# The norm weight of a differential attention: multiplied into the gates, or into half the rows of the output weights

## The chip, the cores and the metric

The kernel runs on one core of a Trainium2 chip. A core has five engines that work side by side and wait for each other through semaphores: TensorE (PE in the profile, its weight loads PEld), VectorE (DVE), ScalarE (ACT), GpSimd (POOL) and SyncE (SP), which here issues nearly all transfers between the chip's memory and the on-chip buffers. The metric is the device time of one execution in microseconds (us), the median over runs; lower is better. Besides, one execution of each kernel was profiled, and its trace lists every instruction.

## The reference, cut to what matters

The reference is one step of a two-layer network on 1280 tokens (256 context, 1024 latent) of width 1024. Layer 0 has a convolution branch A and a differential attention B with 4 heads of 128 value channels; layer 1 has two grouped-query attentions. Each layer is an input projection, its branches, and an output projection. In layer 0 a head's output `o` is normalised over its 128 channels, multiplied by a norm weight `subln_g` (one number for each of the 128 channels, the same for all heads) and a constant, and by a gate of its own:

```
o = over_query_blocks(lambda qb: diff_attend(qb, keys, vals, lam), q)
o = rms_norm(o, subln_g) * (1.0 - lam_init)
o = o.reshape(b, T, B_W) * jax.nn.silu(b_z)
return jnp.concatenate([a, o], axis=-1) @ w_out, new_kv
```

`lam_init` is 0.2 in layer 0. The branches are concatenated, so columns 0 to 511 of the product's left side come from A and columns 512 to 1023 from B, head by head; `w_out` has 1024 rows to match. A factor that depends on the channel alone can therefore stand on the left side's column or on the matching row of `w_out`.

## The kernel before, in words

All work is in tiles of 128 tokens (ten of them, two of context and eight latent). Products that need full precision are made of three matmuls over a high and a low part of each operand; so each weight chunk is loaded, rounded by ACT to its high part, and the rest taken by a subtraction (`wcut`, `wo_chunk`).

**Input projection of layer 0** (`l0_in`, profile about 45 to 530 us). Seven groups of 512 output columns are run one after the other, group by group over the tokens (`run_group`). Four of the groups are heads (`head_units`). For each head and token tile `vz_done` (L507) takes the values and the gate from the product: ACT copies the value (L509), `silu2` makes the gate with a tanh on ACT and one DVE instruction (L339, L340), then DVE multiplies it by the tile `subg` (L513), and SP stores it to the tensor GZ0 in memory (L514). That is 40 times, for 4 heads and 10 tiles. Between the groups' units a filler runs the convolution and then the layer norm of branch A in five pairs of tiles (`ln_steps`, L557 to L598: loads of the convolution's result L569, DVE L574 to L581, POOL L583 and L584, ACT L582 and L585, DVE L586 and L587, store L588), and a second generator works out the next modulations. `subg` is set up once at the start (L1365 to L1367): the norm weight is loaded to all 128 partitions, 128 numbers in each, and multiplied by 0.4 (0.8 for the constant, and a half that `silu2` leaves out).

**First attention** (`l0_attn`, about 514 to 804 us). Its keys and first queries (`l0_keys` L646 to L653, `l0_query` L661) are loaded in the last part of the input projection, after two thirds of the last head's units (`freed0`), into memory that the projection has left. A head's gates come back from GZ0 in one load (L752). In `fin` DVE multiplies the normalised head output by the gate (L724), and SP writes it into the concatenated tensor CAT (L727).

**First output projection** (`out_proj`, about 802 to 955 us). The weights come in eight chunks of 128 rows (`wo_chunk`, L811): SP loads a chunk of 512 KB into a tile `wor` (L815), ACT rounds it half by half (L818), and POOL subtracts (L819). Chunks 0 to 2 are made during the attention, chunks 3 to 7 at the start of the projection (L844) through three slots, so that a further load waits until POOL is done with an earlier chunk. Chunks 4 to 7 are the rows 512 to 1023. The first two token tiles are projected together: for each chunk, PE makes two products with the high part of the token tile, by the weights' high (L852) and low part (L853), and one with its low part (L856). ACT then reads the two accumulators (L870), and POOL and DVE finish the tile. The token tiles are transposed in `prep` (L832 to L835).

**What sets the order.** The program text gives the dependences and a first order; the order in which each engine gets its instructions is then written out by a planner, which simulates the whole program with costs of its own and lets an instruction go when its operands are ready by that simulation (L1547: `schedule_with_timeline_sim=True`). At run time each engine works through its own list in that order; an instruction that has to wait holds up those behind it, and the same holds for the list of transfers that SP issues.

Of the kernel before, what the change touches and what calls it, by code (L numbers as in the profile page):

```python
# [10 lines left out]
F32 = mybir.dt.float32  # L11
# [3 lines left out]
ALU = mybir.AluOpType  # L15
# [17 lines left out]
def f32(ap):  # L33
    return ap.bitcast(F32)
# [42 lines left out]
class K:  # L77
# [323 lines left out]
    def l0_in(self, ws, raw, wp, cxp, p1, small, acc, pst, mod, freed):  # L401
        nc, a = self.nc, self.a
# [80 lines left out]
        def head_units(h):  # L483
# [23 lines left out]
            def vz_done(t, ps):  # L507
                v = small.tile([128, 128], F32, tag="vz", name=f"vz{h}_{t}")
                nc.scalar.copy(v, ps[:, 256:384])  # L509
                nc.sync.dma_start(self.V0[h, t], v)  # L510
                gz = small.tile([128, 128], F32, tag="gz", name=f"gz{h}_{t}")
                self.silu2(gz, ps[:, 384:512], small, f"z{h}_{t}")
                nc.vector.tensor_tensor(gz, gz, self.subg, ALU.mult)  # L513
                nc.sync.dma_start(self.GZ0[h, t], gz)  # L514
                return v

# [294 lines left out]
    def wo_chunk(self, l, k, pool, bufs=1):  # L811
        nc = self.nc
        w = pool.tile([128, 2, D], F32R, name=f"wo{l}_{k}")
        r = pool.tile([128, D], F32, tag="ac", bufs=bufs, name=f"wor{l}_{k}")
        nc.sync.dma_start(r, self.a["wo"][l, k])  # L815
        for n in range(2):
            s = slice(n * 512, n * 512 + 512)
            nc.scalar.copy(w[:, 0, s], r[:, s])  # L818
            nc.gpsimd.tensor_tensor(w[:, 1, s], r[:, s], f32(w[:, 0, s]), ALU.subtract)  # L819
        return w  # L820
# [411 lines left out]
def build(tc, a):  # L1232
    nc = tc.nc
    k = K(tc, a)
    with ExitStack() as ctx:
        cst = ctx.enter_context(tc.tile_pool(name="cst", bufs=1))
# [29 lines left out]
        def pool(c, name, bufs=1, **kw):  # L1266
            return c.enter_context(tc.tile_pool(name=name, bufs=bufs, **T, **kw))
# [41 lines left out]
        with ExitStack() as c1:  # L1309
# [9 lines left out]
            with ExitStack() as c2:  # L1319
                xp = pool(c2, "xp0", 3)  # L1320
                k.cond(cst, xp)

                def load(g):
                    t0, n = TGS[g]
                    xs = []
                    if g == 1:
                        quad = hp.tile([128, 4, D], F32, tag="lo2", name="x0_g1")
                    for t in range(t0 // 128, (t0 + n) // 128):
                        if g == 0:
                            x = xp.tile([128, D], F32, tag="x", bufs=2, name=f"x0_{t}")  # L1330
                        elif g == 1:
                            x = quad[:, t - t0 // 128]
                        else:
                            if t % 2 == 0:
                                pair = hp.tile([128, 2, D], F32, tag=("hi0", "lo0")[t % 4 // 2], name=f"x0_{t}")
                            x = pair[:, t % 2]
                        nc.sync.dma_start(x, a["x"][t])
                        xs.append(x)
                    return xs

                def norm(x, t):
                    junk = xp.tile([128, D], BF16, tag="junk", bufs=1, name=f"xj_{t}")
                    k.x_norm(x, junk, small, f"x{t}")

                xs = load(1)
                first = k.mod_steps(0, (0, 2, 1, 3), xp, wp, "w", small, psm, pst, cst, nc.vector, "xraw")
                for i in range(20):
                    next(first)
                    if i % 5 == 3:
                        norm(xs[i // 5], 2 + i // 5)  # L1350
                k.use_mod()
                k.h_group(0, 1, xs, hpr, xp, pst, range(4))
                for _ in first:
                    pass
                k.after = k.last
                k.h_group(0, 1, xs, hpr, xp, pst, range(4, 8))
                ws = k.wgroup(a["we"][0], raw, wp, "w0")
                with tc.issue_after(k.after):
                    k.ropeC = cst.tile([128, 8, 64], F32, name="ropeC")
                    nc.sync.dma_start(k.ropeC, a["ropec"])  # L1360
                    k.ropeS = cst.tile([128, 8, 64], F32, name="ropeS")
                    nc.sync.dma_start(k.ropeS, a["ropes"])
                    k.ropeT = hp.tile([128, 2, 1024], F32, name="ropeT")
                    nc.sync.dma_start(k.ropeT, a["ropet0"])
                    k.subg = cst.tile([128, 128], F32, name="subg")  # L1365
                    nc.sync.dma_start(k.subg, a["subg"].broadcast_to([128, 128]))
                    nc.vector.tensor_scalar(k.subg, k.subg, 0.4, None, ALU.mult)  # L1367
                    k.nsink = cst.tile([128, 8], F32, name="nsink")
                    nc.sync.dma_start(k.nsink, a["sink"].broadcast_to([128, 8]))
                    nc.vector.tensor_scalar(k.nsink, k.nsink, -1.0, None, ALU.mult)  # L1370
                    k.qn = cst.tile([128, 64], F32, name="qn")
                    nc.sync.dma_start(k.qn, a["qn"].broadcast_to([128, 64]))
                    k.kn = cst.tile([128, 64], F32, name="kn")
                    nc.sync.dma_start(k.kn, a["kn"].broadcast_to([128, 64]))
                    ls = cst.tile([128, 4], F32, name="ls")
                    lam = hp.tile([128, KC, 512], F32, tag="hi2", name="lam")[:, 0, 0:384].rearrange("p (v d) -> p v d", d=64)
                    lv, lp = lam[:, 0:4], lam[:, 4:6]
                    nc.sync.dma_start(lv, a["lamv"][None].broadcast_to([128, 4, 64]))
                    nc.vector.tensor_tensor(lp, lv[:, 0::2, :], lv[:, 1::2, :], ALU.mult)
                    nc.vector.tensor_reduce(ls[:, 0:2], lp, AX.X, ALU.add)  # L1380
                    nc.scalar.activation(ls[:, 0:2], ls[:, 0:2], AF.Exp)
                    k.nlam = ls[:, 3:4]
                    nc.vector.tensor_tensor(ls[:, 2:3], ls[:, 1:2], ls[:, 0:1], ALU.subtract)
                    nc.vector.tensor_scalar(k.nlam, ls[:, 2:3], -0.2, None, ALU.add)
                    for g in (2, 0):
                        xs = load(g)
                        for i, x in enumerate(xs):
                            norm(x, TGS[g][0] // 128 + i)
                        k.h_group(0, g, xs, hp, xp, pst, eng=nc.vector)
# [171 lines left out]
```

## Time and profile before

| | |
|---|---|
| median of 3 runs | 1828.43 us (1823.73 to 1829.55) |
| profiled execution, its own time | 1829.68 us |
| its span, first to last instruction | 1827.9 us |
| PE busy | 1727.2 us, 94% of the span |
| DVE busy | 1238.3 us, 68% |
| ACT busy | 971.6 us, 53% |
| POOL busy | 782.0 us, 43% |
| granted TensorE clock, mean | 0.985 |

Busy time is the time in which an engine had an instruction under way, waiting for a port or a buffer of the on-chip memory included. A row of a group of instructions names the line of the kernel, the engine, the operation, and what is written from what. In rows in order of time the first number is the start in us, the second the duration or, for several of a kind (x2), their common stretch; brackets give the idle time of the engine just before and what ended it.

### The profile page before, as it was taken

To read this page: it belongs to the slowest core of one execution; us is meant where nothing else is said; L and a number is where in the kernel's file an instruction comes from. 1 tells how busy PE (TensorE), PEld (TensorE's weight loads), DVE (VectorE), ACT (ScalarE), POOL (GpSimd) and SP (SyncE) were. 2 spreads that over 40 slices of the span, in tenths; PEclk is the share of its full clock that TensorE was granted. 3 is DMA by queue.
4 is the path that set the end of the run, shared out by engine and by line. 5 is a ranking of instruction groups with operands and counts; after the bars stand their busy time and mean duration, and the time that the engine had idled before them with its cause. 6 is when DMAs were issued, how large, how long until landed. Compare 5 with 4: busy or idle time off the path is not lost. (4 is left out here: it accounts for less than half of the span.)

```text
span 1827.9 us, 28289 instructions
## 1 busy us (share of the span) xinstructions
PE 1727.2 (94%) x9434; PEld 1419.5 (78%) x9434; DVE 1238.3 (68%) x2975; ACT 971.6 (53%) x2040; POOL 782.0 (43%) x696
## 2 busy tenths in 40 slices
PE   6999999999859999899999999998999999999998
PEld 2787788988747777778887778886888888878886
DVE  6657545674779999945566672118899989999322
ACT  6432244344337777753344543217778878898311
POOL 2322022222557777763237873203344334354332
PEclk9999999999979999999999999999999999999999
DMA  8457478785764433144146346254112114141441
GB/s 292 166 161 211 150 185 203 190 234 134 222 185 113 139 104 93 47 137 163 72 156 199 139 121 167 75 137 113 36 43 66 36 41 107 53 146 58 156 173 55
DMA packets 220086, 241.24 MB, mean 132 GB/s; under 512 B 72128, under 2 KB 154464, under 8 KB 219684
## 3 DMA queue, kind: packets, MB, share of 16 engines
q1 hardware_dynamic: 207284, 233.53, 43.1%
q0 software_dynamic: 1792, 3.15, 0.9%
q10 hardware_dynamic: 10864, 2.75, 0.8%
q8 instruction: 75, 1.23, 0.3%
q14 instruction: 71, 0.58, 0.1%
HBM read 169.08 MB, written 70.28 MB: 131 GB/s over the span
## 5 line engine op out<-in xcount | busy, mean ns | idle before, releaser
L397 ACT ACTIVATE E<-E,mm 128x1536 f32<-128x1536 f32 (+3 forms) x240 | 293.5, 1227 | 69.0 <-DVE E L394 58.4
L270 POOL TENSOR_TENSOR w_w<-raw_w,w_w 128x512 fp32r<-128x512 f32 x88 | 118.7, 1360 | 258.1 <-ACT w_w L269 244.0
L1217 PE MATMUL S<-k1d,q1s 128*128 128x512 f32 (+1 forms) x704 | 206.4, 389 | 4.5 <-DMA q1s<-qT 2.1
L372 POOL TENSOR_TENSOR el<-ef,eh 128x512 fp32r<-128x512 f32 x96 | 124.3, 1296 | 185.6 <-DVE eh L371 180.7
L394 DVE TENSOR_SCALAR_CACHE_REDUCE E<-S,mm 128x512 f32<-128x512 f32 x256 | 189.8, 744 | 11.5 <-PE S L777 3.0
L1147 PE MATMUL wt_et<-ident,E 128*128 128x128 f32 x1264 | 186.2, 273 | 3.2 <-ACT E L397 2.5
L1147 PEld LDWEIGHTS wt_et<-ident,E 128*128 128x128 f32 x1264 | 153.6, 140 | 37.3 <-ACT E L397 4.3
L777 PE MATMUL S<-kd,qs 128*128 128x512 f32 (+1 forms) x416 | 133.4, 431 | 30.2 <-DVE E L394 24.1
L368 DVE TENSOR_TENSOR el<-wt_et,eh 128x512 fp32r<-128x512 f32 x220 | 146.8, 682 | 10.0 <-ACT eh L367 9.3
L1217 PEld LDWEIGHTS S<-k1d,q1s 128*128 128x128 f32 x704 | 121.3, 190 | 28.5 <-DVE E L394 7.1
L367 ACT CAST eh<-wt_et 128x512 fp32r<-128x512 f32 x220 | 124.1, 594 | 30.4 <-PE wt_et L1147 29.9
L1142 PE MATMUL pv_pv<-el,v 128*128 128x512 f32 x316 | 138.8, 439 | 0.5 <-POOL el L372 0.2
L318 PE MATMUL acc_g<-w_w,hi 128*128 128x512 f32 x336 | 131.5, 393 | 1.8 <-DVE v L1000 1.3
L319 PE MATMUL acc_g<-w_w,hi 128*128 128x512 f32 x336 | 132.4, 394 | 0.5 <-POOL w_w L270 0.5
L320 PE MATMUL acc_g<-w_w,lo 128*128 128x512 f32 x336 | 131.6, 392 | 0.0
L1141 PE MATMUL pv_pv<-eh,v 128*128 128x512 f32 x316 | 128.3, 406 | 0.9 <-DVE eh L371 0.5
L852 PE MATMUL acc_po<-wo,oh 128*128 128x512 f32 x320 | 126.0, 395 | 0.6 <-DVE oy L724 0.6
L853 PE MATMUL acc_po<-wo,oh 128*128 128x512 f32 x320 | 125.1, 392 | 0.0
L394 DVE TENSOR_SCALAR_CACHE_REDUCE E<-S 128x512 f32<-128x512 f32 (+1 forms) x160 | 99.8, 629 | 18.7 <-PE S L1217 11.7
L777 PEld LDWEIGHTS S<-kd,qs 128*128 128x128 f32 x416 | 70.0, 197 | 51.6 <-DVE E L394 38.6
L856 PE MATMUL acc_po<-wo,ol 128*128 128x512 f32 x320 | 103.3, 393 | 0.0
L269 ACT CAST w_w<-raw_w 128x512 fp32r<-128x512 f32 x96 | 59.0, 621 | 82.8 <-DMA raw_w<-in_wod 23.3
(294 smaller groups left out, 4544.4 us busy)
## 6 DMA issues: line engine op xcount, KB each, us to landing
rawm_v<-in_wmodt SPq DMA_DIRECT2D x64, 256.0 KB, 3.1
raw_w<-in_we SPq DMA_DIRECT2D x56, 256.0 KB, 3.4
X<-AW SPq DMA_DIRECT2D x32, 336.0 KB, 5.5
qs<-QK SPq DMA_DIRECT2D x80, 128.0 KB, 2.8
ac<-CAT SPq DMA_DIRECT2D x20, 512.0 KB, 3.5
raw_w<-in_wod SPq DMA_DIRECT2D x40, 256.0 KB, 2.8
q1s<-qT SPq DMA_DIRECT2D x40, 256.0 KB, 2.6
xraw_m<-in_wmod SPq DMA_DIRECT2D x32, 256.0 KB, 4.8
```

The costliest lines, as they stand in the source:

```text
L318: nc.tensor.matmul(ps[:, o:], a, w[:, 0, o:], start=(k == 0), stop=False)
L319: nc.tensor.matmul(ps[:, o:], a, w[:, 1, o:], start=False, stop=False)
L320: nc.tensor.matmul(ps[:, o:], b, w[:, 0, o:], start=False, stop=(k == KC - 1))
L368: nc.vector.tensor_tensor(lo, ps, f32(hi), ALU.subtract)
L394: nc.vector.tensor_scalar(e[:, o : o + w], S, -1.0, init, ALU.mult, ALU.min, accum_out=m[:, i : i + 1])
L397: nc.scalar.activation(e[:, :n], e[:, :n], AF.Exp, bias=init, scale=-1.0, accum_out=s)
L777: nc.tensor.matmul(S, q[:, hl], kd[:, c, kofs + o : kofs + o + n], start=(hl == 0), stop=(hl == 1))
L852: nc.tensor.matmul(po[hn], oh[:, k, :], wo[k][:, 0, s], start=(k == 0), stop=False)
L1141: nc.tensor.matmul(pv, vs, wh, start=(i == 0), stop=False)
L1142: nc.tensor.matmul(pv, vs, wl, start=False, stop=(i == nk - 1))
L1147: nc.tensor.transpose(ps[:, g * 128 : g * 128 + 128], E[g][:, ec : ec + 128], self.ident)
L1217: nc.tensor.matmul(S, qs[:, g, :], kd[hl][:, kc : kc + n], start=(hl == 0), stop=(hl == 1))
```

## The change

The multiplication of the gates by `subg` is taken out. Instead each of the chunks 4 to 7 of the first output weights is multiplied, after its load and before it is split, by `subg` as one number for each partition (a partition of the chunk is a row of the weights, and so a channel of a head). `subg` becomes a column: 128 partitions with one number each, loaded as such, and still multiplied by 0.4. The stored gates and the head outputs in CAT are without the factor; the product is the same.

```diff
@@ head_units, vz_done
                 self.silu2(gz, ps[:, 384:512], small, f"z{h}_{t}")
-                nc.vector.tensor_tensor(gz, gz, self.subg, ALU.mult)
                 nc.sync.dma_start(self.GZ0[h, t], gz)
@@ wo_chunk
         nc.sync.dma_start(r, self.a["wo"][l, k])
+        if l == 0 and k >= 4:
+            nc.vector.tensor_scalar(r, r, self.subg, None, ALU.mult)
         for n in range(2):
@@ build
-                    k.subg = cst.tile([128, 128], F32, name="subg")
-                    nc.sync.dma_start(k.subg, a["subg"].broadcast_to([128, 128]))
+                    k.subg = cst.tile([128, 1], F32, name="subg")
+                    nc.sync.dma_start(k.subg, a["subg"].rearrange("o p -> p o"))
                     nc.vector.tensor_scalar(k.subg, k.subg, 0.4, None, ALU.mult)
```

## The prediction

> **What bounds the kernel now.** I read the page's span and busy times first, then a table of busy time by stage, and then, for the two stages that the edit touches, the instructions in order of time on each engine. The columns of the stage table are the stretch, its length, then the busy time of PE, PEld, DVE, ACT and POOL (number of instructions in brackets), the granted TensorE clock, the DMA share and GB/s.
>
> ```profile
> span 1827.9 us, 28289 instructions
> PE 1727.2 (94%) x9434; PEld 1419.5 (78%) x9434; DVE 1238.3 (68%) x2975; ACT 971.6 (53%) x2040; POOL 782.0 (43%) x696
> ...
> 250.00:480.00 230.00, 230.00 (x1607) 206.40 (x1606) 138.75 (x284) 98.68 (x252) 65.40 (x50) 1.00 0.72 184
> 480.00:530.00 50.00, 29.51 (x166) 26.19 (x164) 36.45 (x66) 16.34 (x45) 29.26 (x25) 0.80 0.68 212
> ```
>
> TensorE is the bound nearly everywhere, and from 250 to 480 us it has no gap at all: what another engine saves there can't shorten the span. The exception is the seam between the first input projection and the first attention, from 480 us on: 29.51 busy in 50. The gates' multiply (L513) lies across both, and the new multiply lands in the first output projection.
>
> ```profile
> L513 DVE TENSOR_TENSOR gz<-gz,subg x40: 254/291/6066, 259.9 to 519.1; 128x128 f32<-128x128 f32 x40
> ...
> 250.00:480.00 230.00, 17.64 (x34) 1.00 0.72 184
> 480.00:533.00 53.00, 7.33 (x7) 0.79 0.65 205
> ```
>
> The first row has the 40 removed instructions with their shortest, median and longest duration in ns: half of them take 291 or less, one took 6066. The other two are the same instructions by stage (DVE busy): 17.64 us lie under a full TensorE, 7.33 in the seam, 25.0 in all.
>
> **Part 1, the removal under a full TensorE.** 17.64 us of DVE time go from 250 to 480 us. They cost nothing now, because PE is busy 230 of these 230 us (rows above), so they give 0. If that cover were gone they would be worth their 17.64 at most; nothing else in the edit takes it away.
>
> **Part 2, the removal in the seam.** Here are the rows on which it turns, in order of time and from four engines; SPq is the queue of the engine that issues nearly all transfers.
>
> ```profile
> 477.72 6.07 DVE L513 TENSOR_TENSOR gz<-gz,subg 128x128 f32<-128x128 f32 x1
> 478.58 2.55 POOL L583 TENSOR_TENSOR lu<-lu,lncon 128x512 f32<-128x512 f32 x2
> 478.75 1.43 SPq L570 DMA_DIRECT2D azr<-AZ  x1
> 481.09 2.54 POOL L584 TENSOR_TENSOR lu<-lu,lncon 128x512 f32<-128x512 f32 x2
> 482.41 0.63 ACT L585 ACTIVATE lu<-lu 128x512 f32<-128x512 f32 x1 [4.02 <-POOL lu L584]
> 483.71 0.68 DVE L586 SCALAR_TENSOR_TENSOR lu<-lu 128x512 f32<-128x512 f32 x1
> 483.81 0.32 SPq L514 DMA_DIRECT2D GZ<-gz  x1
> 484.22 0.60 SPq L646 DMA_DIRECT2D kd<-QK  x1
> 485.51 0.61 SPq L651 DMA_DIRECT2D ck<-in_cbk  x1
> 489.49 0.68 DVE L495 TENSOR_TENSOR ch<-cn,ropeT 128x512 f32<-128x512 f32 x1
> 492.05 1.29 POOL L653 TENSOR_TENSOR kd<-ck,kd 64x512 fp32r<-64x512 f32 x1 [8.43 <-DMA qs<-QK]
> 493.42 2.50 POOL L499 TENSOR_TENSOR ch<-ch 128x512 f32<-128x512 f32 x2
> 495.38 1.09 DVE L501 TENSOR_TENSOR ch<-ch 128x512 fp32r<-128x512 f32 x1 [5.21 <-ACT ch L500]
> 500.90 1.12 PE L360 MATMUL tr_st<-ident,hl 128*128 128x128 f32 x4 [6.42 <-DVE hl L357]
> 505.23 1.06 DVE L513 TENSOR_TENSOR gz<-gz,subg 128x128 f32<-128x128 f32 x1
> 514.53 1.37 DVE L513 TENSOR_TENSOR gz<-gz,subg 128x128 f32<-128x128 f32 x1
> 517.31 0.85 SPq L569 DMA_DIRECT2D lu<-CV  x2
> 520.10 1.37 DVE L574 SCALAR_TENSOR_TENSOR lu<-lu,lncon 128x512 f32<-128x512 f32 x2 [0.74 <-DMA lu<-CV]
> 532.92 7.23 PE L777 MATMUL S<-kd,qs 128*128 128x512 f32 x18 [16.99 <-DVE E L394]
> ```
>
> The 6.07 us instruction needs no data after 477.7; it ends at 483.79, when POOL's four two-input instructions end (481.09+2.54 = 483.63). DVE gains little when it goes: the next one, L586, needs ACT's L585, done at 482.41+0.63 = 483.04, so at most 0.67 us. SP gains more: its store of that gate (L514) stands in line until 483.81, though SP was free from 478.75+1.43 = 480.18. Behind it stands the 1280 KB load of the keys (L646), which can start up to 3.6 us earlier, and with it out of the way the small load behind it (ck, L651) lands sooner. POOL waits 8.43 us for that load, and the chain that ends PE's 6.42 us gap hangs on POOL: L653, L499, ACT's L500, DVE's L501 and what DVE has queued behind it, then the transposes of L360. From the same DVE queue the layer norm's pairs go on to the last loads of the convolution (L569), and to the 16.99 us gap.
>
> ```profile
> ck<-in_cbk SPq DMA_DIRECT2D x8, 128.0 KB, 4.7
> kd<-QK SPq DMA_DIRECT2D x4, 1280.0 KB, 8.3
> ```
>
> The price: ck took 492.05-485.51 = 6.54 us until POOL could go, against a median of 4.7 for all eight such loads (last column, us to landing), so 1.8 us is the value taken. The bounds are 0 (the queue stays as full) and 3.2: L499 can't start before DVE's L495 ends at 489.49+0.68 = 490.17, and it started at 493.42. Of the later L513 the one at 505.23 costs the chain about 0.3 us (estimate: a plain one is 0.29); the one at 514.53 delays a pair whose successor waits for a store anyway (0.74 us idle before L574). Sum for the seam: -2.1, from 0 to -3.5.
>
> **Part 3, the new multiply.** Four 128x1024 DVE instructions with one column as scalar now stand between the landing of weight chunks 4 to 7 and ACT's copy. Nearest row: L221, the same form and shape.
>
> ```profile
> L221 DVE TENSOR_SCALAR xr<-xr,ss_n x10: 745/753/1861, 834.1 to 941.2; 128x1024 f32<-128x1024 f32 x10
> ...
> 804.62 1.37 SPq L815 DMA_DIRECT2D wor<-in_wo  x3
> 808.70 1.14 ACT L818 CAST wo<-wor 128x512 fp32r<-128x512 f32 x2 [6.17 <-DMA wor<-in_wo]
> 809.45 12.59 POOL L819 TENSOR_TENSOR wo<-wor,wo 128x512 fp32r<-128x512 f32 x10 [5.96 <-ACT wo L818]
> 812.01 2.83 SPq L815 DMA_DIRECT2D wor<-in_wo  x2
> 818.78 1.14 ACT L818 CAST wo<-wor 128x512 fp32r<-128x512 f32 x2 [1.31 <-DMA wor<-in_wo]
> 822.44 1.29 DVE L835 TENSOR_TENSOR ol<-tr_cT,oh 128x512 fp32r<-128x512 f32 x2 [18.30 <-ACT oh L834]
> 822.29 0.40 PE L852 MATMUL acc_po<-wo,oh 128*128 128x512 f32 x1
> 822.52 0.40 PE L853 MATMUL acc_po<-wo,oh 128*128 128x512 f32 x1
> 824.57 0.60 ACT L870 ACTIVATE oj<-acc_po 128x512 bf16<-128x512 f32 x1 [1.67 <-PE acc_po L856]
> ```
>
> One takes 0.75 us, and up to 1.86 beside POOL. DVE has room: it is idle for 18.30 us before 822.44, so nothing is queued behind the new waits but that L835, which is later. What isn't free is the chain of each chunk: load, multiply, ACT, POOL. POOL's ten subtractions of five chunks run without a break from 809.45 to 822.04, and PE uses the last half from about 822.52. If each multiply holds POOL off for its own 0.75 us, the run ends 4 x 0.75 = 3.0 later. Chunks 4 and 5 land while POOL works on chunk 3, but a lock still holds POOL; for chunk 7 ACT starts at 818.78 and POOL only gets to it at 822.04-2 x 1.26 = 819.5 (12.59 for ten), so there 0.7 us is slack. PE can take other products of the two first tiles while it waits: between 822.04 and 824.57, when ACT can read the first result, it has some ten matmuls left at 0.23 us from start to start (822.29 to 822.52), of which two at least need the last half, so about 8 x 0.23 = 1.8 us of the 3.0 is hidden (estimate). Value taken: +1.2. Bounds: 0 (all hidden by slack and order) and +3.6: a multiply of 1.86 on chunk 4 holds POOL, the slot of chunk 7 comes free 1.9 us later (three slots, L815 twice at 812.01 after POOL's chunks), and its own multiply of 1.86 on the path, less the 0.1 that ACT and POOL overlap.
>
> What the Trainium skill says of this, "SBUF — State Buffer", section "Who interferes with whom": a DVE instruction with two SBUF inputs, or a tensor_scalar in a two-port mode, and a GpSimd instruction that reads SBUF exclude each other, and whoever starts first holds the pair for that whole instruction. By that rule a multiply waits for at most one POOL subtraction, so 0.75+1.26 = 2.01 at worst, and the 1.86 of L221 agrees; the 6.07 of L513 doesn't, since it outlasted four POOL instructions. By the rule Part 3 stays at +1.2, by the 6.07 row a multiply could wait out a whole run of POOL, but here POOL runs dry two subtractions later, because its next chunk needs the multiply.
>
> **Part 4, the column load.** The norm weight comes as 128 single numbers instead of 128 rows of 512 bytes, and its scaling is 128x1. No row shows so narrow a load; DVE waited 1.13 us for the old one, and was idle later for 2.89 us until another load of the same group.
>
> ```profile
> 48.27 0.23 DVE L1367 TENSOR_SCALAR subg<-subg 128x128 f32<-128x128 f32 x1 [1.13 <-DMA subg<-in_subg]
> 51.53 0.29 DVE L1379 TENSOR_TENSOR lam<-lam 128x128 f32<-128x128 f32 x1 [2.89 <-DMA lam<-in_lamv]
> ```
>
> So a landing up to 2.9 us later is covered by the wait before 51.53, and one that is earlier only moves that wait. Value 0, bounds -0.1 and +0.5 (the nearest row, the old load of the same column count, is where I stay).
>
> **The sum**: 0 - 2.1 + 1.2 + 0 = -0.9 us. The profiled execution took 1829.68 us (span 1827.9 and 1.8 around it), so 1828.8 for a profile after. That execution lies 1.25 above the median of the three runs, 1828.43; for the median the forecast is 1828.43 - 0.9 = 1827.5. A difference under 0.3% (5.5 us; the three runs before spread over 5.8) can't be told from none, so this is "no change".
>
> One thing no row prices: the order of instructions on every engine is written by a planner from its own simulated times, and with 40 instructions fewer it may draw the seam differently. Where PE has no gap this matters little; in the seam PE is idle for 20.5 of the 50 us, and both rivals with a visible result live there.
>
> **Rivals.**
>
> Faster (chance 0.23): the seam is one chain through DVE, and the stalled time of L513 comes off in full. Three of its instructions there took 6.07, 1.06 and 1.37; less a plain 0.29 each that is 7.6, and the seven in the seam's stretch are worth 0.29 each, 2.0. Then -9.6 + 1.2 = -8.4, about 1820.0. For it: PE's two gaps (6.42 and 16.99) both end on DVE. Against: after the longest stall DVE is idle for 5.21 us until ACT's L500, so that stall isn't what ends last there.
>
> Slower (0.19): a gate store no longer holds SP back, so the key load, ready since long, is put or drifts ahead of the convolution's loads (L569) in the last pairs. These are needed at once (DVE idle 0.74 before L574); behind a transfer that takes 8.3 us instead of landing in 2.8 (517.31 to 520.10) they come 5.5 later, PE's 16.99 us gap grows by as much, and with Part 3: +5.5 + 1.2 = +6.7, about 1835.1. It decides as soon as the last L569 load lands over 1 us later against the last matmuls of the input projection than now. For it: the key load was held by exactly such a store. Against: it is issued before the loads in question already, and starting sooner frees the DMA engines sooner.
>
> Weight chain (0.14): the multiplies hold POOL in full and PE waits for the last half (+3.6), and the seam gives nothing: 1832.0, still within what can't be told.
>
> Forecast (0.44): -0.9, its own range 1823 to 1831.
>
> **How the numbers follow.** Within 0.3%: the forecast, the weight chain but for 0.01 each side, so 0.56; faster 0.24; slower 0.20. Eight in ten from the faster rival less 2 (1818) to the slower one plus 2 (1837).
>
> **What would show it.** L513 gone, L340 kept at 40; SP's key load in the seam issued some 3 us earlier before the same point of PE's work; POOL's 8.43 us wait shorter by 1 to 3; PE's two gaps of 6.42 and 16.99 together 1 to 3 us less. In the output projection four DVE multiplies of 0.75 to 1.9 us, POOL's ten subtractions spread over some 15 us instead of 12.59, PE idle there up to 3 us more. It would be wrong if the gaps of the seam change by over 6 us in sum, if PE shows a gap outside these two places that it didn't have, or if one multiply takes more than 2.6 us.

## The result, and the profile after

The changed kernel took 1839.26 us in the median of 6 runs (1835.07 to 1841.81), against 1830.25 us for the kernel before (6 runs, 1823.73 to 1833.19). The ratio is 1.0056, with a 95% interval from 1.0042 to 1.007: some 10 us slower. The forecast of 1827.5 us ("no change") was wrong, and the time lies above its range, too. The profiled execution after took 1835.07 us. It is the fastest of the six, so its trace shows only some 5 of the 10 us (spans 1833.3 against 1827.9). Ratios, here and below, are taken over runs in the same clock state (one run of 1931 and one of 2715 us in the experiments, at granted clocks of 0.84 and 0.58, are left out) and are not exactly the quotient of the two medians.

The page of the changed kernel, first the span and the busy times, then the two stretches of the stage table in the columns used above (length, busy PE, PEld, DVE, ACT, POOL, granted clock, DMA share, GB/s):

```profile
span 1833.3 us, 28260 instructions
PE 1729.7 (94%) x9434; PEld 1418.6 (77%) x9434; DVE 1227.7 (67%) x2939; ACT 972.5 (53%) x2040; POOL 783.9 (43%) x696
```

```profile
250.00:480.00 230.00, 226.78 (x1594) 203.19 (x1594) 124.62 (x246) 96.44 (x247) 58.38 (x44) 1.00 0.75 182
480.00:530.00 50.00, 32.16 (x178) 28.28 (x176) 36.19 (x62) 18.03 (x49) 31.66 (x28) 0.84 0.76 224
```

DVE is 10.6 us less busy. By the 25.0 us that went and the 6.1 of the four new multiplies (rows below) it would be 18.9, so its other instructions took some 8 us more in this trace. TensorE, with the same 9434 matmuls, is 2.5 us busier, and from 250 to 480 us, where it had no gap before, 3.2 us of it are idle now. The changed kernel's list of waits of PE between 300 and 480 us shows two releasers that were not there (total, times, longest, in us):

```profile
PE tr_st L360 <- DVE hl L357: 1.5, 1, 1.5
PE tr_cv L471 <- DVE cy L477: 1.3, 2, 1.0
```

In the seam the rows that answer to those of before are these, from SP, POOL and PE (the lines 513 to 815 of the kernel before are one lower after, those from 816 up one higher):

```profile
484.02 0.46 SPq L513 DMA_DIRECT2D GZ<-gz  x1
484.57 0.60 SPq L645 DMA_DIRECT2D kd<-QK  x1
485.22 0.61 SPq L650 DMA_DIRECT2D ck<-in_cbk  x1
494.60 1.29 POOL L652 TENSOR_TENSOR kd<-ck,kd 64x512 fp32r<-64x512 f32 x1 [4.30 <-DMA ck<-in_cbk]
507.82 1.11 PE L360 MATMUL tr_st<-ident,hl 128*128 128x128 f32 x4 [10.13 <-DVE hl L357]
537.64 7.24 PE L776 MATMUL S<-kd,qs 128*128 128x512 f32 x18 [15.36 <-DVE E L394]
```

By the clock the key load is issued no earlier (484.57 against 484.22), and a gate store stands ahead of it in SP's list as before. But PE comes to the first of its two gaps 3.2 us later than before (507.82 - 10.13 = 497.7 against 500.90 - 6.42 = 494.5). Against PE's work, then, the load is issued some 2.8 us earlier, and POOL's wait is shorter, 4.30 against 8.43. So far Part 2 came true. Yet the two gaps of PE have together 25.5 us, against 23.4: the first is 3.7 us longer, the second 1.6 shorter.

The gain was lost further down the same chain, at the end of which PE waits for DVE's L357, and L357 for ACT's L356. Before, L356 was done at 500.39 and L357 started at 500.42. After, in the planner's new order, the layer norm's L573, which waits 0.81 us for a load of the convolution's result, stands ahead of L357:

```profile
504.55 0.40 ACT L356 CAST hl<-nat 128x256 fp32r<-128x256 f32 x1
505.67 0.69 DVE L573 SCALAR_TENSOR_TENSOR lu<-lu,lncon 128x512 f32<-128x512 f32 x1 [0.81 <-DMA lu<-CV]
506.40 1.36 DVE L357 TENSOR_TENSOR hl<-nat,hl 128x256 fp32r<-128x256 f32 x1
```

That is a loss of 1.4 us (from 504.95 to 506.40); 0.9 more come from L357 itself (1.36 against 0.42), and some 2.0 were lost before, between POOL's start and DVE's gate instruction L340 (8.8 us against 6.8).

In the first output projection, first the start of PE before, then the rows after:

```profile
801.88 0.48 PE L852 MATMUL acc_po<-wo,oh 128*128 128x512 f32 x1
```

```profile
804.43 0.48 PE L853 MATMUL acc_po<-wo,oh 128*128 128x512 f32 x1
811.87 8.44 POOL L820 TENSOR_TENSOR wo<-wor,wo 128x512 fp32r<-128x512 f32 x6 [5.83 <-ACT wo L819]
812.48 2.94 DVE L816 TENSOR_SCALAR wor<-wor,subg 128x1024 f32<-128x1024 f32 x2 [5.79 <-DMA wor<-in_wo]
819.13 1.74 DVE L816 TENSOR_SCALAR wor<-wor,subg 128x1024 f32<-128x1024 f32 x1 [3.71 <-POOL wo L820]
821.60 5.46 POOL L820 TENSOR_TENSOR wo<-wor,wo 128x512 fp32r<-128x512 f32 x4 [1.29 <-ACT wo L819]
822.06 1.38 DVE L816 TENSOR_SCALAR wor<-wor,subg 128x1024 f32<-128x1024 f32 x1 [1.20 <-DMA wor<-in_wo]
828.22 0.60 ACT L871 ACTIVATE oj<-acc_po 128x512 bf16<-128x512 f32 x1 [1.69 <-PE acc_po L857]
```

Here things went as forecast: four multiplies of 1.4 to 1.7 us, and POOL's ten subtractions over 15.2 us (811.87 to 827.06). The projection's first matmul started at 801.88 before and at 804.43 after, so from there to ACT's first read it is 23.8 us against 22.7: +1.1.

What no part of the forecast speaks of is TensorE's rate in layer 1. Here are three products, each in the same stretch of its own trace (shortest/median/longest in ns): the one with the normed input's low part in layer 1's input projection (L320), and in the last output projection the one with the weights' low part (L853, after the change L854) and the one with the token tile's low part (L856, then L857). Before:

```profile
L320 PE MATMUL acc_g<-w_w,lo x147: 387/389/397, 1103.5 to 1209.4; 128*128 128x512 f32 x147
L853 PE MATMUL acc_po<-wo,oh x109: 389/389/395, 1719.9 to 1799.6; 128*128 128x512 f32 x109
L856 PE MATMUL acc_po<-wo,ol x108: 389/389/476, 1720.6 to 1799.2; 128*128 128x512 f32 x108
```

After:

```profile
L320 PE MATMUL acc_g<-w_w,lo x138: 389/395/398, 1108.2 to 1209.4; 128*128 128x512 f32 x138
L854 PE MATMUL acc_po<-wo,oh x106: 389/396/398, 1720.6 to 1799.6; 128*128 128x512 f32 x106
L857 PE MATMUL acc_po<-wo,ol x107: 389/395/480, 1719.8 to 1799.8; 128*128 128x512 f32 x107
```

The median instruction is some 6 ns longer, hundreds of microseconds away from anything that the edit does. What did change for them is where their operands lie. `subg` was a tile of 512 bytes in each partition and became one of 32 (4 bytes, padded). The tiles of the left side of the on-chip memory are stacked behind it, and in the compiled program 2850 of 2976 tiles have moved down by 480 bytes; those allocated from the right side have not. Start addresses modulo 256:

```
tile                                          before   after
normed input, layer 1, token groups 0, 1        224       0
the same, token group 2 (right side)            224     224
input weights, layer 1 (right side)             224     224
output weights, layer 1, chunks 0 to 5 (right)  224     224
output weights, layer 1, chunks 6, 7            224       0
output weights, layer 0, chunks 0 to 2 (right)  224     224
output weights, layer 0, chunks 3 to 7          224       0
token tiles of both output projections, 0 and 1 224     224
the same, tiles 2 and later                     224       0
normed input, layer 0, groups 0, 2              224       0
input weights, layer 0                          128     160
X, image of the convolution (layer 0)           128     160
```

The changed kernel's own trace has a comparison in it: in layer 1's input projection the products of token group 2, whose two operands still start alike, follow each other at 0.227 us in the median, those of groups 0 and 1 at 0.233; before, all at 0.227. So the theory to test was A: a matmul is slower when the starts of its stationary and its moving operand differ modulo some power of two. The rival B: places don't matter, and the planner's other order, or the new work itself, costs the 10 us. It was A with an addition that only the experiments forced, D.

### The profile page after: what moved, and what is told of

It is laid out like the page before. It is cut to its first block, busy times and chain, and to the rows that moved or that the text cites. A ratio compares the mean times of both kernels' runs of the same rounds, so it can differ in the third digit from the quotient of the medians.

```text
span 1833.3 us, 28260 instructions
## 1 busy us (share of the span) xinstructions
PE 1729.7 (94%) x9434; PEld 1418.6 (77%) x9434; DVE 1227.7 (67%) x2939; ACT 972.5 (53%) x2040; POOL 783.9 (43%) x696
## 5 line engine op out<-in xcount | busy, mean ns | idle before, releaser
L368 DVE TENSOR_TENSOR el<-wt_et,eh 128x512 fp32r<-128x512 f32 x220 | 147.1, 683 | 10.2 <-ACT eh L367 9.9
L320 PE MATMUL acc_g<-w_w,lo 128*128 128x512 f32 x336 | 132.7, 395 | 0.0
L853 PE MATMUL acc_po<-wo,oh 128*128 128x512 f32 x320 | 126.5, 398 | 0.6 <-DVE oy L723 0.6
L854 PE MATMUL acc_po<-wo,oh 128*128 128x512 f32 x320 | 126.6, 396 | 0.0
L394 DVE TENSOR_SCALAR_CACHE_REDUCE E<-S 128x512 f32<-128x512 f32 (+1 forms) x160 | 99.9, 630 | 16.3 <-PE S L1218 10.6
L857 PE MATMUL acc_po<-wo,ol 128*128 128x512 f32 x320 | 104.1, 396 | 0.0
```

The costliest lines, as they stand in the source:

```text
L320: nc.tensor.matmul(ps[:, o:], b, w[:, 0, o:], start=False, stop=(k == KC - 1))
L368: nc.vector.tensor_tensor(lo, ps, f32(hi), ALU.subtract)
L394: nc.vector.tensor_scalar(e[:, o : o + w], S, -1.0, init, ALU.mult, ALU.min, accum_out=m[:, i : i + 1])
L854: nc.tensor.matmul(po[hn], oh[:, k, :], wo[k][:, 1, s], start=False, stop=False)
```

## Experiments

All edits are to the changed kernel or to the kernel before, as said; times are medians, the ratio is to the kernel before on the same chip. In all of them that differ from one of the two only in places, the order of instructions on every engine is that kernel's.

**The change with its tiles in the old places.** Instead of 32 bytes the column gets the old tile's 512:

```diff
-                    k.subg = cst.tile([128, 1], F32, name="subg")
+                    subg = cst.tile([128, 128], F32, name="subg")
+                    k.subg = subg[:, 0:1]
```

> The changed kernel, but the column of the norm weight is the first of 128 columns of a tile as large as before (512 bytes in each partition), so that every tile behind it lies where it lay before the change. The instructions and their order on each engine are those of the changed kernel. Theory A (places): the small tile moved all tiles on one side of the memory by 480 bytes, an odd multiple of 32, and TensorE's matmuls whose two operands now start in different halves of 64 bytes follow each other at 0.232 to 0.235 us instead of 0.227; with the old places this goes, some 6 to 7 us by the two traces, and what is left is the order and the new multiply: 1831 to 1834 us. Theory B (order): the planner's new order costs the time, and the places nothing: 1839 us, as the changed kernel.

Measured: 1832.29 us, ratio 1.0011 (1.0001 to 1.0021). The same row of layer 1 is back at the time of before:

```profile
L320 PE MATMUL acc_g<-w_w,lo x148: 387/390/397, 1103.3 to 1209.9; 128*128 128x512 f32 x148
```

So of the 10 us some 8 belong to the places alone; the edit itself, new order included, costs about 2.0 (0.2 to 3.8).

**The kernel before, moved.** Its `subg` tile made larger by 32, and by 64 bytes in each partition (`[128, 136]` and `[128, 144]`, of which the first 128 numbers are used):

> The kernel before, with its tile of the norm weight 32 bytes wider, which nothing reads; instructions and order are those of the kernel before, and all tiles behind it lie 32 bytes higher. Theory A (places): slower by 6 to 7 us, 1836 to 1838, with the dense matmuls of the second layer's projections at 0.232 to 0.235 us from start to start where their stationary operand has moved and 0.227 where it has not. Theory B (order): as before, 1830.

> As the run with 32 bytes, but 64 bytes wider: all tiles behind it lie 64 bytes higher. Theory A (places), in the form that only the half of 64 bytes counts: as before, 1830. If any move of the tiles counted, or their exact places, it would be slower as well, 1836 or more. Theory B (order): as before, 1830.

Measured: 1837.49 us, ratio 1.0036 (1.0021 to 1.0051), and 1837.74 us, 1.0043 (1.0029 to 1.0058). Not an instruction is different, and some 7 us are gone. The form in which 64 bytes would be a whole period fell.

**The removal alone.** L513 taken out of the kernel before and nothing put in its place; it leaves out the norm weight and the factor 0.4, its tiles stand in the old places, and the planner's order is its own:

```diff
-                nc.vector.tensor_tensor(gz, gz, self.subg, ALU.mult)
```

> The kernel before without the gates' multiply, and with nothing in its place: the norm weight and its 0.4 are left out of the computation. Tiles lie as before; the planner draws an order of its own. By the prediction's part 2 the removal alone is worth 2.1 us (0 to 3.5): 1828. Theory A: no part of the loss comes from here, 1825 to 1832. Theory B (order): the order drawn without the multiplies costs time by itself, 1836 or more.

Measured: 1831.57 us, ratio 1.0003 (0.9989 to 1.0016). The 40 instructions are worth nothing that can be measured; the -2.1 of Part 2 lies just outside this interval (-2.0 to +2.9 us). In its trace, too, and in that of the run with old places, PE's two gaps of the seam are no shorter than before: 24.4 and 24.5 us, against 23.4.

**Making the first projection's operands equal, too.** If A was the whole story, there was something to gain in layer 0, where the weights started at 128 and the normed input at 224 already before the change. 96 unused bytes ahead of the weights make them equal; first in the changed kernel with old places, then in the kernel before:

```diff
+            pool(c1, "gap0").tile([128, 24], F32, name="gap0")
             wp = pool(c1, "wp0")
```

> The changed kernel with its column in a tile of 512 bytes per partition (so every tile stands where it stood before the change) and 96 unused bytes ahead of the weight ring of the first input projection, so that these weights start at 224 modulo 256 as the normed input does (before: 128 against 224). Theory A (matmuls slow by some 3% when the starts of stationary and moving operand differ modulo 128 or 256): the roughly 1280 dense matmuls of the first projection that now follow each other at 0.234 us go to 0.227, up to 9 us, less what a bound other than TensorE takes back there: 1823 to 1828 against 1832.3 for the same kernel without the 96 bytes. Rival C (it was not the difference of the starts, but only the particular places of layer 1's tiles): 1832, no change.

> The kernel before with nothing but the same 96 unused bytes ahead of the weight ring of the first input projection; instruction order as before. Theory A: the same 4 to 9 us come off, 1821 to 1826. Rival C: 1830.

Measured: 1835.24 us, ratio 1.003 (1.0017 to 1.0043), and 1837.57 us, 1.0027 (1.0011 to 1.0044). Both slower, where A had promised 4 to 9 us off; rival C had said no change, so both expectations missed. And yet the matmuls did what A says: in the second kernel's trace those of layer 0 follow each other at 0.227 us instead of 0.234. The gain was lost in a gap. Rows of the kernel before with the 96 bytes, in order of time:

```profile
356.59 0.70 DVE L162 CUSTOM_DVE_ANT_0 md_v<-rawm_v,cr(0, 2)_1_2388 128x512 f32<-128x512 f32 x1 [4.95 <-DMA rawm_v<-in_wmodt]
360.10 1.26 DVE L477 TENSOR_TENSOR cy<-tr_cv,cy 42x256 f32<-42x256 f32 x2
360.82 1.41 PE L471 MATMUL tr_cv<-band_band,X 128*42 128x64 f32 x16 [3.42 <-DVE cy L477]
364.11 0.63 PE L319 MATMUL acc_p<-w_w,hi 128*128 128x512 f32 x1
365.18 0.39 PE L319 MATMUL acc_p<-w_w,hi 128*128 128x512 f32 x1
```

DVE waits 4.95 us for a load of modulation weights; behind it in its queue stands L477, which frees the accumulator that PE's next convolution block needs; PE stands still for 3.42 us, and then its matmuls take 0.63 us instead of 0.39 for a while. The transfers were late, though nothing was loaded that was not loaded before. From 250 to 480 us the share of DMA time is 0.77 instead of 0.72, at fewer GB/s (181 against 184), and this view of one load's transfers (x times, KB, median us from issue to landing) names the one that had changed. Kernel before, and then the kernel before with the 96 bytes:

```profile
X<-AW SPq DMA_DIRECT2D x32, 336.0 KB, 5.5
```

```profile
X<-AW SPq DMA_DIRECT2D x32, 336.0 KB, 6.5
```

X is the convolution's image. It is loaded in pieces of 64 numbers, 256 bytes, 1344 of them in each load, and the 96 bytes had moved X from 128 to 224. From here theory D: two costs of place, that of A, and a second one, of 256-byte pieces that take longer where X has an unfavourable start, so that in layer 0's projection transfers come too late for PE.

**By 128 and by 256 bytes.** To tell the period, the kernel before was moved up by 128 bytes (as shown) and by 256 (`[128, 192]`):

```diff
-                    k.subg = cst.tile([128, 128], F32, name="subg")
+                    subg = cst.tile([128, 160], F32, name="subg")
+                    k.subg = subg[:, 0:128]
```

> The kernel before with the norm weight's tile 128 bytes larger per partition, so every tile of the left side stands 128 bytes higher; order as before. Theory A with a period of 128 bytes: 1830, as before. Theory A with a period of 256: 1836 to 1838, as with 32 and 64 bytes. Rival C (any other place than the one before costs): 1836 to 1838.

> The kernel before with the norm weight's tile 256 bytes larger per partition, so every tile of the left side stands 256 bytes higher; order as before. Theory A: 1830 with either period, since every difference of starts is what it was modulo 256. Rival C: 1836 to 1838.

Measured: 1829.06 us, ratio 0.9999 (0.9987 to 1.0012), and 1829.11 us, 1.0 (0.9983 to 1.0018). By what was expected the first would speak for a period of 128. It doesn't: in its trace the matmuls whose starts differ by 128 follow each other at 0.232 us, as slow as others, so the period is 256. The loss was paid back elsewhere: X starts at 0 there, its loads land in 5.1 us instead of 5.5, and the first projection is 2.7 us shorter (table below). A time alone would have led astray here.

**X back, all else as changed; all else back, X not.** In the changed kernel 224 unused bytes ahead of the convolution's pool bring X to 128 again; in the changed kernel with old places 32 bytes (8 numbers in place of the 56 shown) bring X to 160:

```diff
+            pool(c1, "gap1").tile([128, 56], F32, name="gap1")
             cxp = pool(c1, "cx0")
```

> The changed kernel with 224 unused bytes ahead of the convolution's tiles, so that X, into which the transfers of the convolution's image go in pieces of 256 bytes, starts at 128 modulo 256 as in the kernel before (changed: 160); the operands of layer 1's projections and of the output projections stay unequal, instruction order as changed. Theory D (two placement costs: unequal matmul operands, some 3 us, and 256-byte pieces that land in X off a multiple of 128, some 4 us, through the first projection's transfers): 1834 to 1836 against 1839.3. Theory A alone (only the matmul operands): 1838 to 1840.

> The changed kernel with every tile where it stood before the change, except the convolution's tiles, which stand 32 bytes higher (X at 160 modulo 256 instead of 128). Theory D: the 256-byte pieces take some 27 ns instead of 23, the first projection gets its gaps, 1835 to 1838 against 1832.3 for the same kernel with X at 128. Theory A alone: 1831 to 1834.

Measured: 1836.41 us, ratio 1.0037 (1.0022 to 1.0052), and 1841.51 us, 1.0061 (1.0039 to 1.0082). The first lies between the two ranges, and its interval (some 1833 to 1839 us) touches both, so this time alone doesn't decide; the second is beyond A's range by some 7 us, on the side of D. With X back the changed kernel's L357 wait of 1.5 us ahead of PE's transposes is gone, while one of 1.1 at L471 stays, and its layer 1 is as slow as ever; a row of the last output projection of the changed kernel with X back:

```profile
L854 PE MATMUL acc_po<-wo,oh x105: 389/396/398, 1720.0 to 1798.5; 128*128 128x512 f32 x105
```

**X alone, its neighbours alone.** The pool holds other tiles beside X (the bands, the results `cy`, the keys' and queries' `ch`). In the changed kernel with old places, X alone goes to 160 (as shown: 32 bytes ahead of it, and behind it 224, which bring the neighbours back to 128); then the neighbours alone (only 32 bytes behind X); then X alone in the kernel before:

```diff
+            cxp.tile([128, 8], F32, tag="gx", bufs=1, name="gx")
             xs = [windows(0)]
+            cxp.tile([128, 56], F32, tag="gy", bufs=1, name="gy")
```

> The changed kernel with every tile where it stood before the change, except X alone, which starts at 160 modulo 256 instead of 128 (its neighbours in the pool, the bands, the results cy and the keys' and queries' tiles ch, stay at 128). Theory D in the form that X carries the cost: 256-byte pieces at 26 to 28 ns, 1834 to 1842 (the pool as a whole gave 1841.5). In the form that a neighbour carries it: 1831 to 1834, as with all at 128 (1832.3).

> The opposite: X at 128 as before the change, its neighbours in the pool (bands, cy, ch) at 160. If X carries the cost: 1831 to 1834. If a neighbour does: 1836 to 1842.

> The kernel before, order as before, with X alone at 160 modulo 256 instead of 128. If X carries the cost, as in the kernel before with all of the left side 32 bytes up (1837.5, of which some 3 us belong to the matmuls of layer 1): 1833 to 1838. Otherwise 1829 to 1831.

Measured: 1835.85 us, ratio 1.0037 (1.0022 to 1.0051); 1832.03 us, 1.0016 (1.0 to 1.0031); 1833.67 us, 1.0031 (1.0017 to 1.0045). X carries the cost, not its neighbours. The loads of X, then the stage table, with X alone at 160:

```profile
X<-AW SPq DMA_DIRECT2D x32, 336.0 KB, 6.5
```

```profile
250.00:480.00 230.00, 227.13 (x1586) 204.13 (x1585) 124.92 (x247) 96.86 (x247) 58.23 (x44) 0.99 0.75 181
```

The same two with the neighbours alone at 160:

```profile
X<-AW SPq DMA_DIRECT2D x32, 336.0 KB, 5.7
```

```profile
250.00:480.00 230.00, 227.96 (x1592) 204.01 (x1591) 126.83 (x247) 98.10 (x249) 59.77 (x45) 1.00 0.72 182
```

**Everything even.** The 96 bytes ahead of the first projection's weights and 32 ahead of the convolution's pool, so that all operands of the dense products start at 224 and X at 0:

```diff
+            pool(c1, "gap0").tile([128, 24], F32, name="gap0")
             wp = pool(c1, "wp0")
...
+            pool(c1, "gap1").tile([128, 8], F32, name="gap1")
             cxp = pool(c1, "cx0")
```

> The changed kernel with tiles where they stood before, but 96 unused bytes ahead of the first projection's weights (their start equal to that of the normed input, 224 modulo 256) and 32 ahead of the convolution's tiles (X at 0 modulo 256). Theory D: matmuls of the first projection at 0.227 us and 256-byte pieces at some 19 ns; the 96 bytes alone gave 1835.2 with X at 224, so 4 to 9 us come off that and off 1832.3: 1823 to 1829. Theory A alone: as with the 96 bytes, 1835.

> The kernel before with the same 96 and 32 unused bytes; order as before. Theory D: 1820 to 1826 against 1829 to 1830. Theory A alone: as with the 96 bytes alone, 1837.

Measured: the changed kernel so placed 1826.39 us, ratio 0.9983 (0.9968 to 0.9998), the kernel before so placed 1823.97 us, 0.9972 (0.9959 to 0.9985). Both beat both kernels of this study, the second by 5.3 us for 128 bytes of unused memory; the very 96 bytes that cost time when X went to 224 with them (1.0027) are part of it once X is at 0. In the first of them PE's first projection is full again, at the faster rate (its own rows: stage, then a line of layer 0's products, 391/397/632 ns in the kernel before):

```profile
250.00:480.00 230.00, 229.84 (x1609) 208.05 (x1608) 128.24 (x251) 99.04 (x252) 65.54 (x51) 1.00 0.70 186
```

```profile
L319 PE MATMUL acc_az<-w_w,hi x80: 387/389/628, 167.8 to 239.5; 128*128 128x512 f32 x80
```

The row of the kernel before that this answers to:

```profile
L319 PE MATMUL acc_az<-w_w,hi x80: 391/397/632, 170.4 to 241.3; 128*128 128x512 f32 x80
```

The profiled executions, but for that of the removal alone, side by side: us from one matmul to another of the same number in TensorE's order (the order differs between the upper and the lower half, the stages don't), with the places in which they differ ("equal": stationary against moving, modulo 256):

```
                            X mod  equal in  equal in   first input   layer 1's    last output
kernel                       256   layer 0   layer 1    projection    input proj.  projection
                                                        (300-2400)    (5100-6000)  (9000-9433)
changed                      160   no        in part      356.5         200.7        94.7
 X back                      128   no        in part      354.4         200.7        94.7
 old places                  128   no        yes          356.3         199.1        92.6
 old, neighbours at 160      128   no        yes          356.7         199.1        92.6
 old, X alone at 160         160   no        yes          360.8         199.1        92.6
 old, whole pool at 160      160   no        yes          360.8         199.1        92.6
 old, 96 bytes               224   yes       yes          356.8         199.1        92.6
 everything even               0   yes       yes          350.8         199.1        92.6
before                       128   no        yes          353.2         199.1        92.6
 32 up                       160   no        in part      359.2         200.7        94.7
 64 up                       192   no        in part      358.0         200.7        94.6
 128 up                        0   no        in part      350.5         200.5        94.4
 256 up                      128   no        yes          354.0         199.1        92.6
 X alone at 160              160   no        yes          357.3         199.1        92.6
 96 bytes                    224   yes       yes          360.4         199.1        92.6
 everything even               0   yes       yes          347.8         199.1        92.6
```

The last two columns show the matmul cost, with only two levels in sixteen executions (128 bytes up lies just under the upper one): +1.6 and +2.1. They cover a part of the matmuls concerned. Over the whole of the first output projection, layer 1's input projection and the last output projection (matmuls 4153 to 4744, 4748 to 6113, 8890 to 9433) the executions with equal operands there (the removal alone is one) average 123.5, 303.6 and 115.9 us, those with partly unequal ones 124.4, 306.3 and 117.9: together some 5.6 us, though in the first of the three the two groups overlap. The times of X back and of old places, which have the same order of instructions and X at 128 both, are 1.0037 - 1.0011 apart, 4.8 us (some 1.5 to 8). The column of the first projection follows X: within the lower half 348 to 351 with X at 0, 353 to 354 at 128, 357 to 360 else; in the upper half 351, 354 to 357 and 356 to 361, so that there the last two touch.

## Why the prediction was wrong, step by step

**Part 4 is the step that failed.** "Value 0, bounds -0.1 and +0.5" prices the new column as a transfer. As a transfer it was right: DVE waited 0.31 us for it instead of 1.13, and the later wait stayed (2.83 against 2.89). Rows after:

```profile
47.89 0.15 DVE L1368 TENSOR_SCALAR subg<-subg 128x1 f32<-128x1 f32 x1 [0.31 <-DMA subg<-in_subg]
...
51.07 0.29 DVE L1380 TENSOR_TENSOR lam<-lam 128x128 f32<-128x128 f32 x1 [2.83 <-DMA lam<-in_lamv]
```

But a tile is also a place, and 480 bytes less of it moved nearly every tile of the kernel. That has two prices that the sum didn't have: some 4.8 us of slower matmuls in layer 1 and both output projections (X back, 1.0037, against old places, 1.0011), and some 3.5 us from X (1.0056 less 1.0037). With the edit's own 2.0 they make the 10.2 us, as differences of the same ratios must. The 3.5 is by itself not clear of noise; that X's place costs time is shown by X alone at 160, which took 4.8 us more than old places and 5.7 more than the kernel before.

**Part 1** said that the removal under a full TensorE is worth 0, which the run without L513 bears out, and that "nothing else in the edit takes [the cover] away", which was wrong. The full 230 us looked like a stage with TensorE as its only limit. It was a stage in which the transfers had just enough slack. In the changed kernel the loads of X land 0.8 us later (its row of them, against 5.5 in the median before), and gaps open:

```profile
X<-AW SPq DMA_DIRECT2D x32, 336.0 KB, 6.3
```

Over all seventeen traces PE's idle time from 250 to 480 us is 0.0 to 0.2 us with X at 0, 0.0 to 2.0 with X at 128, and 1.6 to 5.5 with X at 160, 192 or 224. So the kernel before, with none, was lucky for a kernel with X at 128: moved by 256 bytes, with the same instructions and all starts alike modulo 256, it has 1.2.

**Part 2** (-2.1) came true in its first half only. The key load goes out 2.8 us earlier against PE's work, and POOL waits 4.1 us less (Part 2's row names a load of the queries, `qs`, as what ended that wait, where the text reads `ck`; the row after names `ck`). But the rest of the chain, from POOL to DVE's L357, was redrawn and took longer: PE's gaps of the seam are 2.1 us longer instead of shorter, and the removal alone gives 1.0003. That the planner might redraw the seam was said and put into the rivals; the step itself took DVE's list from the old trace as if it were kept.

**Part 3** was right: +1.1 against +1.2, multiplies of 0.75 to 1.86 forecast and 1.38 to 1.74 seen, POOL's run 15.2 us against "some 15". From the Trainium skill, "SBUF — State Buffer", section "Who interferes with whom", it was taken there that a multiply waits for one subtraction of POOL at most, 2.01 us in all; the trace agrees, with 1.74 for the longest.

**The rivals.** The slower one gave the right sign and 1835.1, by another mechanism: the last load of L569 was issued 1.5 us ahead of PE's second gap (520.79), where before it came 1.4 us into it (517.31). Of the marks that were named for "wrong", one came true: gaps of PE outside the two places, L471 and L360 between 300 and 480 us. The busy time of PE, +2.5 us for the same matmuls, was the mark of the larger cost, and it wasn't on the list.

**What stays open.** The costs don't add up in every run: in the kernel before, 32 bytes up gives 6.6 us, less than X alone (5.7) and the matmuls (4.8) together; the whole pool at 160 gave 1.0061, X alone 1.0037 and the neighbours alone nothing (the intervals of the first two overlap), and 1841.5 lies 3.5 us above the range expected. The first projection is where loads and TensorE meet, and what is late there depends on more than one of them. Why an operand's start matters to a matmul was not tried beyond its size; nor how much of the edit's 2 us belongs to the new order.

## What to carry to other kernels

Changing the size of a long-lived tile moves every tile stacked behind it: before pricing an edit, look at the start addresses of the operands of the dense matmuls and of tiles that are loaded in small pieces, and keep the old size, or pad, so that they don't change. A stage with a full TensorE may still have a second limit right behind it; here the DMA share of the stage told how near: at 0.69 and 0.70 PE was idle there for 0.2 us at most, at 0.72 for 0.0 to 2.0, at 0.74 to 0.77 for 1.6 to 5.5. The median landing time of X told less: it was 5.7 us in one kernel with 0.2 us of idle time and in another with 2.0. And where an edit that only moves things around changes busy time for the same instructions, compare durations line by line far away from the edit first.

## What was unexpected of the hardware

**Matmuls.** Dense 128x128 by 512 products in the full-precision format of this kernel, from start to start, in fourteen of the executions: 0.227 us where stationary and moving operand start at the same address modulo 256 (27830 matmuls), 0.232 to 0.234 in the median at differences of 32, 64, 96, 128 and 160 (18077 matmuls with any difference; 0.233 over all), 0.230 and 0.234 at 192 and 224:

```
difference mod 256     0      32      64      96     128     160     192     224
matmuls            27830    3481    1818    7170    1181    2758     713     956
median us          0.227   0.233   0.233   0.234   0.232   0.232   0.230   0.234
```

The products of the attentions showed no such difference: the scores of layer 1 (L1217 of the kernel before) follow each other at 0.234 us with equal starts and at 0.233 to 0.235 at differences of 32, 64 and 128.

**256-byte pieces into the on-chip memory.** Mean time of one such packet on a DMA engine's queue of loads (43264 in each execution, nearly all of them X's): 18.9 to 19.2 ns with X at 0 modulo 256, 22.1 to 23.6 at 128, 26.4 to 27.6 at 160, 192 and 224. The Trainium skill, "DMA: Bandwidth & Descriptors", section "How a descriptor splits into AXI transactions", says that the first transaction of a piece that doesn't start on a multiple of 256 bytes begins at the boundary below. By that a piece of 256 bytes takes two transactions instead of one. The trace agrees that 0 is cheapest; that 128 is cheaper than the rest doesn't follow from that rule, and the section speaks of reading while X is written.

**The clock after a gap.** After PE's gap of 3.42 us in the kernel before with 96 bytes, which ended at 360.82, the granted clock was 0.50 from 361.50 to 364.91, and 1.00 then (stretches of 3.0 and 5.0 us of that kernel, columns as in the stage table):

```profile
361.90:364.90 3.00, 3.00 (x15) 2.78 (x14) 3.00 (x10) 1.89 (x6) 0.00 (x0) 0.50 0.87 252
365.00:370.00 5.00, 5.00 (x40) 4.55 (x39) 3.24 (x9) 0.74 (x2) 1.28 (x1) 1.00 0.86 185
```

By an estimate from these figures that gap cost 3.4 us and half of the 3.4 at half the clock, about 5.1. The Trainium skill, "TensorE: Matmul & The Clock Gate", Part 1, has the clock halved after an idle window of about 3.4 us and until a busy one of the same length; this trace agrees (3.42 us of gap, 3.41 at 0.50).
